# MLP of an encoder trunk in fp32: the up projection as seven block products on 256 tokens each, weight sums by accumulating DMAs, one block seeded in its PSUM bank

## The chip, the cores and the metric

One core of a Trainium2 chip. The time is that of one execution on the device in microseconds; lower is better. The kernel works in fp32: a product of fp32 numbers is made from three TensorE passes on rounded parts (fp32r): high x high, high x low, low x high.

## What is computed

Two layers of a bidirectional encoder, 512 tokens, width 1024, hidden width 4096. The part that the change concerns is the last line of a layer, with `hn` the normed input:

```python
hn = rms_norm(x, ln2[l])
x = x + jnp.square(jax.nn.relu(hn @ w_up[l])) @ w_down[l]
```

`hn @ w_up` is 512 x 1024 by 1024 x 4096, `@ w_down` 512 x 4096 by 4096 x 1024. Ahead of it in a layer stand the input projection, the three branches and the output projection `wo`; behind the last layer a final norm.

## The kernel before

**Splitting.** Weights come from DRAM in chunks of 128 x 1024 (512 KB). `wsplit` makes the two parts of a chunk: ScalarE casts it to `wh` (line 242), VectorE subtracts that from it into `wl` (line 243). There are three pairs of buffers `wh`/`wl` (`WB`). Activations are split in the same way by `split` (lines 307 and 308).

**MLP.** The hidden width is worked on in four quarters of 1024 (`qd`). A quarter has an up stage and a down stage.

- *Up*: for each of 8 tiles of 128 features, 8 k-tiles x 3 matmuls of 512 tokens (`proj`, lines 248 to 250), weights as the stationary operand, from tile `wr` (two buffers). ScalarE takes relu from PSUM (line 1319) and squares (line 1320).
- *Down*: the product is cut into 2 x 2 blocks (tokens, k, features) and made from seven block products instead of eight (a Strassen-Winograd scheme): `seven`, called with the numbers 1, 2, 6, 7, 5, 4, 3. Each has 4 k-tiles x 2 token tiles x 3 matmuls of 512 columns (lines 466 to 468). It needs sums of the activations' blocks, which `left_first`, `left_second` and `left_sums` make on VectorE during the up stage, and sums of weight blocks, made on VectorE: four in `early_sums` (lines 450 and 452), four in `seven` (lines 479 and 481). A quarter's weights lie in ten buffers of the pool `wq` (`uload`, line 228).
- The results of down are summed over quarters: 1 and 2 are read apart from banks "c" and "m", 1, 6, 5, 3 add up in "c", 7 and 4 in "a". `on` in `down` adds them to `acc` in SBUF (line 522), and in the last quarter to the residual `xr` (line 516), times r2 or -r2, the square of the norm's factor (relu and square let that factor be applied afterwards).

**Start of the MLP.** Transposes of the residual give the normed input by features (`norm_tok`, `turn`). The first three feature tiles begin on the first four k-tiles, so that the second half of the transposes comes among them.

**Order.** A scheduler places each instruction on its engine's queue by program order among what is ready, with `hp()` as a higher class; `tc.issue_after` fixes an order by hand. Engines run their queues in order. SP issues the loads of weights, POOL the DMAs of activations. Pools are opened and closed (`begin`, `end`) on the same memory: `wq` and `mlp` lie where `Y1` and `Y2` were, and `Y2` holds the operand of `wo`.

**Block products elsewhere.** The input projection uses `seven` too, with `uload` and `early_sums`.

Of the kernel before, what the change touches and what calls it, by code (L numbers as in the profile page):

```python
# [12 lines left out]
P = 128  # L13
S = 512
# [37 lines left out]
def _chunk_keys():  # L52

    res = []
    for l in range(DEPTH):
# [23 lines left out]
def trunk(tc, x0v, xT, xt, ws, fnb, bsb, snk, wst, rope, cmask, amask, ident, out):  # L79
# [4 lines left out]
    def pool(**kw):  # L84
# [18 lines left out]
             "h": 22}  # L103

    HOME = {t: p for p, ts in {"G": ("xs", "zt"), "Y1": ("yh",), "br": ("q", "a", "ao", "g", "ch"), "Y2": ("yi", "th", "mg"), "mlp": ("h",)}.items() for t in ts}
# [3 lines left out]
    WR, WB, NZ, NCT, NSM, NQ = 2, 3, 3, 4, 3, 10  # L109
# [110 lines left out]

    def uload(*key):

        raw = []
        for i in range(10):
            t = part["wq"].tile([P, CW], F32, tag="wq", bufs=NQ, name=nm("wq"))
            if i < 8:
                with hp():
                    d = nc.sync.dma_start(t, ws[CHUNK[key + (i // 2, i % 2)]])
                    if key == (0, "un", 0):
                        last_u[0] = d  # L230
            raw.append(t)
        return [raw[2 * q:2 * q + 2] for q in range(5)]
# [119 lines left out]
    def norm_tok(which, l, xr, keep, unit=1.0):  # L352
# [9 lines left out]
        def turn(fl, ts, banks="ssss"):  # L362
# [3 lines left out]
            for d in range(4 * fl, 4 * fl + 4):  # L366
                if n.xs[d] is None:
                    n.xs[d] = (T("x", "xh", F32R), T("x", "xl", F32R))
                    if keep:
                        n.xf[d] = Z() if d < 4 else T("l", "xf")  # L370
# [3 lines left out]
                src = pt[:, 0:w]  # L374
                parts = [x[:, c0:c0 + w] for x in n.xs[d]]
                if keep:
                    xf = n.xf[d][:, c0:c0 + w]
                    nc.scalar.activation(xf, src, AF.Copy, scale=ln_ap(which, l, d))
                    split(xf, *parts)
                else:  # L380
                    split(src, *parts, ln_ap(which, l, d))
# [23 lines left out]
    def left_first(new, u):  # L405

        p1 = new().rearrange("p (a b) -> p a b", a=2)
        split(u[:, 0:HT], p1[:, 0], p1[:, 1])
        sb_ = part["wq"].tile([P, 2, HT], F32, tag="sf", bufs=2, name=nm("sf"))
        i = nc.vector.tensor_tensor(sb_[:, 0], u[:, 0:HT], u[:, HT:], ALU.subtract)  # L410
        return {"i": i, 1: (p1[:, 0], p1[:, 1]), "u": u, "s": sb_}

    def left_second(new, h, v):
        V = nc.vector
        u, sb_ = h.pop("u"), h.pop("s")
# [1055 lines left out]
```

## Time and profile before

| | |
|---|---|
| median of 3 runs | 1628.48 us (1628.19 to 1629.73) |
| profiled execution | 1628.61 us, span 1626.8 us |
| granted TensorE clock | 0.997 |
| TensorE busy | 1606.8 us, 99% |
| VectorE busy | 1283.3 us, 79% |
| ScalarE busy | 993.3 us, 61% |
| POOL busy | 127.0 us, 8% |
| MLP of layer 0 | from 495.8 to 808.4 us of the span |
| MLP of layer 1 | from 1306.1 to 1618.6 us |

In the profile PE is TensorE's matmul, PEld its weight load, DVE is VectorE, ACT is ScalarE, SP and POOL issue DMAs. A matmul's duration (379 ns for 512 columns) holds the pipeline's depth; what it costs in a row is the distance from start to start. A row of operations gives line, engine, operation, output from inputs, count and the durations in ns (least, median, most, or the mean). In the table by stretch each engine has busy time and count of instructions; behind them stand the granted clock, the DMA engines' share and GB/s.

### The profile page before, as it was taken

The page shows a single profiled execution, that of the slowest core. Times are in us where ns is not written, and L with a number is a line of the kernel's source. Part 1 is how long each engine was busy: PE and PEld are TensorE (multiplying, and loading weights), DVE is VectorE, ACT ScalarE, POOL GpSimd, SP SyncE. Part 2 cuts the span into 40 slices and gives each one's busy share as a digit, 9 for nine tenths or more (in the row PEclk, how much of TensorE's full clock was granted, in tenths as well). Part 3 has the DMA queues.
Part 4 walks back from the last instruction along what each step waited for, and adds up shares of the span by engine and source line. Part 5 has one row for each costly group of instructions (what it writes and reads, how often), then busy time and mean ns, then how long its engine had stood idle before and what let it go on. Part 6 is the DMA issues. An engine that isn't in the chain of part 4 may idle for free.

```text
span 1626.8 us, 21854 instructions
## 1 busy us (share of the span) xinstructions
PE 1606.8 (99%) x8034; PEld 1413.0 (87%) x8034; DVE 1283.3 (79%) x1984; ACT 993.3 (61%) x1695; POOL 127.0 (8%) x185
## 2 busy tenths in 40 slices
PE   9999999999999999999999999999999999999998
PEld 8888888898888888888888888988888888888886
DVE  7996998685666768696989969977956677686967
ACT  7676678685245665545766667787852465545464
POOL 1021000001310000000010210000103000000000
PEclk9999999999999999999999999999999999999999
DMA  9342221222645323332423422212227453332321
GB/s 337 118 151 95 95 78 53 93 95 90 229 170 205 104 104 104 104 106 101 143 98 122 169 96 79 90 53 85 98 89 252 152 194 104 104 109 99 125 70 52
DMA packets 57115, 195.84 MB, mean 120 GB/s; under 512 B 7504, under 2 KB 7888, under 8 KB 57008
## 3 DMA queue, kind: packets, MB, share of 16 engines
q1 hardware_dynamic: 45216, 156.03, 27.7%
q0 software_dynamic: 11648, 38.15, 6.8%
q8 instruction: 63, 1.03, 0.3%
q14 instruction: 44, 0.36, 0.1%
q10 hardware_dynamic: 144, 0.26, 0.0%
HBM read 175.54 MB, written 18.87 MB: 120 GB/s over the span
## 4 chain that ended last, share of the span: by engine, by line
PE 74%; DVE 12%; issue 7%; ACT 5%; POOL 1%; DMA 1%; SPq 0%; POOLq 0%; DVEq 0%; ACTq 0%
PE up L249 7%; PE up L250 7%; PE up L248 7%; PE dA L466 3%; PE dA L468 3%; PE dA L467 3%; DVE ex L667 2%; DVE wl L243 2%; PE wo L300 2%; PE wo L299 2%; PE wo L301 2%; PE dC L466 2%; PE dC L467 2%; PE dC L468 2%; PE po L1109 2%
## 5 line engine op out<-in xcount | busy, mean ns | idle before, releaser
L242 ACT CAST wh<-wq 128x1024 fp32r<-128x1024 f32 x201 | 210.3, 1047 | 169.8 <-PE dA L467 43.0
L243 DVE TENSOR_TENSOR wl<-wq,wh 128x1024 fp32r<-128x1024 f32 x201 | 244.3, 1220 | 86.0 <-ACT wh L242 85.1
L243 DVE TENSOR_TENSOR wl<-wr,wh 128x1024 fp32r<-128x1024 f32 x166 | 203.3, 1225 | 127.8 <-ACT wh L242 122.4
L242 ACT CAST wh<-wr 128x1024 fp32r<-128x1024 f32 x166 | 173.4, 1045 | 208.5 <-PE up L249 57.8
L248 PE MATMUL up<-xh,wh 128*128 128x512 f32 x512 | 194.2, 379 | 0.0
L249 PE MATMUL up<-xl,wh 128*128 128x512 f32 x512 | 194.0, 379 | 0.0
L250 PE MATMUL up<-xh,wl 128*128 128x512 f32 x512 | 193.1, 379 | 0.0
L250 PEld LDWEIGHTS up<-xh,wl 128*128 128x128 f32 x512 | 96.8, 189 | 13.7
L248 PEld LDWEIGHTS up<-xh,wh 128*128 128x128 f32 x512 | 96.8, 189 | 13.7
L249 PEld LDWEIGHTS up<-xl,wh 128*128 128x128 f32 x512 | 96.8, 189 | 13.7
L466 PE MATMUL dA<-wh,sh 128*128 128x512 f32 x256 | 97.1, 379 | 0.0
L467 PE MATMUL dA<-wh,sh 128*128 128x512 f32 x256 | 97.0, 379 | 0.0
L468 PE MATMUL dA<-wl,sh 128*128 128x512 f32 x256 | 90.3, 379 | 0.0
L667 DVE TENSOR_TENSOR ex<-ex 128x512 f32<-128x512 f32 x112 | 79.2, 725 | 2.7 <-ACT key L647 2.7
L625 PE MATMUL at<-qt,kt 128*128 128x128 f32 x448 | 66.5, 281 | 3.9 <-DVE qt L640 2.0
L625 PEld LDWEIGHTS at<-qt,kt 128*128 128x128 f32 x448 | 60.7, 196 | 6.5 <-issue 3.1
L639 ACT ACTIVATE qt<-ex 128x512 f32<-128x512 f32 x56 | 37.5, 670 | 35.5 <-DVE ex L667 24.6
L307 ACT CAST sh<-sf 128x512 fp32r<-128x512 f32 x64 | 39.6, 619 | 24.8 <-DVE sf L430 17.7
L468 PEld LDWEIGHTS dA<-wl,sh 128*128 128x128 f32 x256 | 48.4, 189 | 6.8
L466 PEld LDWEIGHTS dA<-wh,sh 128*128 128x128 f32 x256 | 48.4, 189 | 6.8
L467 PEld LDWEIGHTS dA<-wh,sh 128*128 128x128 f32 x256 | 48.4, 189 | 6.8
L248 PE MATMUL gz<-xh,wh 128*128 128x512 f32 x128 | 49.3, 385 | 0.3 <-DVE gz L804 0.3
(417 smaller groups left out, 4297.9 us busy)
## 6 DMA issues: line engine op xcount, KB each, us to landing
wr<-in_ws_dram SPq DMA_DIRECT2D x166, 512.0 KB, 3.2
wq<-in_ws_dram SPq DMA_DIRECT2D x117, 512.0 KB, 4.3
thd<-zt POOLq DMA_DIRECT2D x32, 256.0 KB, 2.6
th<-thd POOLq DMA_DIRECT2D x32, 256.0 KB, 3.1
mgd<-mg POOLq DMA_DIRECT2D x16, 256.0 KB, 2.4
mB<-mgd POOLq DMA_DIRECT2D x16, 256.0 KB, 4.7
xt<-in_xt_dram SPq DMA_DIRECT2D x8, 256.0 KB, 7.5
xr<-in_xt_dram POOLq DMA_DIRECT2D x8, 256.0 KB, 4.9
```

The costliest lines, as they stand in the source:

```text
L242: cast_i[0] = nc.scalar.copy(hi, raw)
L243: nc.vector.tensor_tensor(lo, raw, hi.bitcast(F32), ALU.subtract)
L248: nc.tensor.matmul(o, whi, xh, start=first, stop=False)
L249: nc.tensor.matmul(o, whi, xl, start=False, stop=False)
L250: return nc.tensor.matmul(o, wlo, xh, start=False, stop=last)
L307: nc.scalar.copy(hi, src)
L466: nc.tensor.matmul(o, xh[:, t], h, start=start and k == 0, stop=False, skip_group_check=True)
L467: nc.tensor.matmul(o, xl[:, t], h, start=False, stop=False, skip_group_check=True)
L468: return nc.tensor.matmul(o, xh[:, t], l_, start=False, stop=k == 3, skip_group_check=True)
L625: nc.tensor.matmul(pt[:, c], kk(st), qq[:, c], start=True, stop=True)
L639: nc.scalar.activation(qt.rearrange(shp, b=nb, h=2), e_q, AF.Exp)
L667: nc.vector.tensor_tensor(o_ap, o_ap, ap_of(ex, i_, [[istep, 2]] + z), ALU.add)
```

## The change

- **Up** becomes block products too (`up` and `block_products` in place of the eight feature tiles; `seven` stays for the input projection). Blocks are 256 tokens x 512 k x 512 features. A product has 4 k-tiles x 4 feature tiles x 3 matmuls of 256 columns, the weights stationary. Its order is 7, 1, 2, 6, 5, 3, 4 (in a layer's first quarter 1, 7, 2, 6, 5, 3, 4). `w_up` is stored in chunks by blocks.
- **Activations.** The normed input gets its block sums in `put_x` and `sum_x`, once a layer. The up stage's `on` makes the four blocks of the hidden activations, and with product 4 the sums that down needs (`half`).
- **Weight sums**: a quarter's stage has a `Unit` with tiles b11, t3, b21, b22 (8 chunks; t3 has four buffers, the others two). t3 is loaded as b12 and has b22 added by a DMA on POOL's queue that accumulates in place; later steps add b11 to t3 (after 7), b12 to b11 and b21 to t3 (after 6). In up, except for the first quarter, the first two are accumulating DMAs; in down and in the first up stage b11 is added to t3 by VectorE and b12 to b11 by DMA. The third is VectorE's in all.
- **Seeded bank**: ScalarE copies product 1 from bank "c" to "m", and product 2 adds to it there.
- **Down**: its order is 1, 2, 7, 6, 5, 3, 4 (1, 2, 7, 6, 5, 4, 3 in the last quarter). `acc` goes: every quarter adds its products to `xr`.
- **Loads**: the next unit's chunks are loaded during this one, as buffers come free. Layer 1's first eight chunks are loaded behind the last down of layer 0 and their `early_sums` moves behind the end of the MLP.

```diff
-            res += [(l, "up", qd, f) for f in range(8)]
+            res += [(l, "up", qd, q, i) for q in range(4) for i in range(2)]
...
+        def add(self, what, q):
+            with hp():
+                for i in range(2):
+                    nc.gpsimd.dma_start(self.t[what][i], self.chunk(q, i), accum_op=ALU.add)
...
+    BANK = {1: "c", 2: "m", 7: "a", 6: "c", 5: "c", 3: "c", 4: "a"}
+    READ = {1: "P1", 2: "P12", 7: "P7", 6: "P16", 5: "P165", 3: "P1653", 4: "P74"}
+
+    def block_products(unit, order, product, on, nxt=None, by_dma=False, between=None, apart=False):
...
+        for n in order:
+            tag = BANK[n]
+            if n in (1, 7):
+                open_(tag)
+            raw = w[{1: "b11", 2: "b21", 7: "t3", 6: "t3", 5: "b11", 3: "b22", 4: "t3"}[n]]
+            pts, hl = banks[tag], []
+            tail = apart and n == order[-1]
+            for s_ in range(2):
+                with hp():
+                    hl.append(wsplit(raw[s_]))
+                if not tail:
+                    with tc.issue_after(turned.ins) if turned else contextlib.nullcontext():
+                        for p in range(2):
+                            mm = product(n, pts[p], p, (2 * s_, 2 * s_ + 1), hl[s_], n in (1, 7))
+                turned = between(mm) if between and n == order[0] and s_ == 0 else None
+            with hp():
+                if n == 7:
+                    if by_dma:
+                        unit.add("t3", 0)
+                    else:
+                        for i in range(2):
+                            V.tensor_tensor(w["t3"][i], w["t3"][i], w["b11"][i], ALU.add)
+                        unit.add("b11", 1)
+                elif n == 1 and by_dma:
+                    unit.add("b11", 1)
+                elif n == 6:
+                    for i in range(2):
+                        V.tensor_tensor(w["t3"][i], w["t3"][i], w["b21"][i], ALU.add)
+            if nxt:
+                for what in {order[2]: ("t3",), 6: ("b21",), 5: ("b11",), 3: ("b22",)}.get(n, ()):
+                    nxt.load(what)
...
+                    if n == 1:
+                        if p == 0:
+                            open_("m")
+                        nc.scalar.copy(banks["m"][p], pts[p])
+                    else:
+                        on(READ[n], p, pts[p])
...
+            r = r2 if sign > 0 else nr2
+            V.scalar_tensor_tensor(xr[t][fl], pt, r[:, t:t + 1], xr[t][fl], ALU.mult, ALU.add)
...
+    def up(qd, unit, nxt, xo, between):
...
+            for k in ks:
+                xh, xl = (ap_of(x, 0, [[1, P], [P, 2]]) for x in xo[k][n])
+                for j in range(2):
+                    c = (k % 2) * S + (2 * p + j) * P
+                    c = slice(c, c + P)
+                    o = by_two(pt[:, j * HT:(j + 1) * HT])
+                    nc.tensor.matmul(o, hl[0][:, c], xh, start=start and k + j == 0, stop=False, skip_group_check=True)
+                    nc.tensor.matmul(o, hl[0][:, c], xl, start=False, stop=False, skip_group_check=True)
+                    i = nc.tensor.matmul(o, hl[1][:, c], xh, start=False, stop=k == 3, skip_group_check=True)
...
+            elif which == "P74":
+                a21, a22, a11, a12 = (u[i, p] for i in (21, 22, 11, 12))
+                V.tensor_tensor(nat(a21), nat(a21), srt(pt), ALU.add)
+                A.activation(a21, a21, AF.Relu)
+                square(a21)
+                V.tensor_tensor(a22, a22, a21, ALU.subtract)
+                V.tensor_tensor(a21, a11, a21, ALU.subtract)
+                half(7, p, a21)
+                V.scalar_tensor_tensor(a11, a22, -1.0, a11, ALU.mult, ALU.subtract)
+                half(6, p, a11)
+                half(5, p, a22)
+                V.scalar_tensor_tensor(a12, a12, -1.0, a11, ALU.mult, ALU.subtract)
+                half(3, p, a12)
...
+        def sum_x():
+            V = nc.vector
+            for d in range(4):
+                u, v = xf[d], xf[d + 4]
+                a11, a21, a12, a22 = u[:, 0:HT], u[:, HT:], v[:, 0:HT], v[:, HT:]
+                sa = T("h", "sa")
+                V.tensor_tensor(sa[:, 0:HT], a22, a21, ALU.subtract)
+                V.scalar_tensor_tensor(sa[:, HT:], sa[:, 0:HT], -1.0, a11, ALU.mult, ALU.subtract)
+                a_ = T("x", "xh", F32R), T("x", "xl", F32R)
+                split(sa, *a_)
...
+                V.scalar_tensor_tensor(sd, a12, -1.0, sa[:, HT:], ALU.mult, ALU.subtract)
+                xo[d][3] = two(xb[d], 1)
+                split(sd, *xo[d][3])
```

More of the change, by code (lines that the diff above doesn't have):

```diff
@@ L447, in early_sums @@
     def early_sums(raw):
-        b11, b12, b22, b21, t1 = raw
+        b11, b12, b22, b21 = raw
+        t1 = [part["G"].tile([P, CW], F32, tag="t1", bufs=2, name=nm("t1")) for _ in range(2)]
+        raw.append(t1)
         for i in range(2):
@@ new lines, in down, with product @@
+    def down(qd, unit, nxt, hs, xr, r2, nr2, done, last):
+        V = nc.vector
+        def product(n, pt, p, ks, hl, start):
+            t = slice(p * P, (p + 1) * P)
+            for k in ks:
+                xh, xl = hs[k][n]
+                c = (k % 2) * S
+                o, h, l_ = by_two(pt), pairs(hl[0], c), pairs(hl[1], c)
+                nc.tensor.matmul(o, xh[:, t], h, start=start and k == 0, stop=False, skip_group_check=True)
+                nc.tensor.matmul(o, xl[:, t], h, start=False, stop=False, skip_group_check=True)
+                i = nc.tensor.matmul(o, xh[:, t], l_, start=False, stop=k == 3, skip_group_check=True)
+            return i
@@ L524, in down @@
-        if qd == 3:
-            for fl in range(2):
-                for t in range(4):
-                    V.scalar_tensor_tensor(xr[t][fl], acc[t][fl], r2[:, t:t + 1], xr[t][fl], ALU.mult, ALU.add)
-        seven(raw, hs, "d", on, apart=last and qd == 3)
+            r = r2 if sign > 0 else nr2
+            V.scalar_tensor_tensor(xr[t][fl], pt, r[:, t:t + 1], xr[t][fl], ALU.mult, ALU.add)
+            if qd == 3 and which in ("P12", "P165", "P74", "P1653"):
+                done(t, fl)
+        order = (1, 2, 7, 6, 5, 4, 3) if qd == 3 else (1, 2, 7, 6, 5, 3, 4)
@@ L1252, in trunk, with rest_of_norm @@
         begin("mlp")
+        unit = Unit(l, "up", 0)
+        for what in ("b11", "t3", "b21", "b22"):
+            unit.load(what)
+        def rest_of_norm(mm):
+            with hp():
+                with tc.issue_after(mm.ins):
+                    tp = n2.turn(1, range(4), "ssaa")
+                n2.end()
+                sum_x()
+            return tp
         last = l + 1 == DEPTH
         Z4("u")
-        n1 = norm_tok("ln1", l + 1, xr, True, 1.0 / math.sqrt(D) if last else 1.0)
-        acc = [[T("tv", "acc"), T("tv", "acc")] for _ in range(4)]
+        n1 = norm_tok("ln1", l + 1, xr, None, 1.0 / math.sqrt(D) if last else 1.0)
         fn_t, held = [], []
@@ L1332, in trunk @@
                         nc.sync.dma_start(fn_t[fl], bass.AP(tensor=fnb.tensor, offset=fnb.offset + fl * S, ap=[[0, P], [1, S]]))
-                else:
-                    nxt = uload(l + 1, "un", 0)
-            down(qd, raw, hs, acc, xr, r2, nr2, done, last)
+            down(qd, unit, nxt, hs, xr, r2, nr2, done, last)
+            unit = nxt
+        if not last:
+            nxt = uload(l + 1, "un", 0)
         if not last:
```

235 lines of the change are left out of this document (139 added, 96 removed).

## The prediction

> **What bounds the kernel now.** I read the page's first and fourth parts first, then a table of busy time by stretch of the MLP, then costs of single operations, then queues.
>
> ```profile
> span 1626.8 us, 21854 instructions
> PE 1606.8 (99%) x8034; PEld 1413.0 (87%) x8034; DVE 1283.3 (79%) x1984; ACT 993.3 (61%) x1695; POOL 127.0 (8%) x185
> PE 74%; DVE 12%; issue 7%; ACT 5%; POOL 1%; DMA 1%; SPq 0%; POOLq 0%; DVEq 0%; ACTq 0%
> ```
>
> TensorE is busy throughout and holds 74% of the chain that ends last; so matmul time taken away counts, if nothing else becomes late. Whether it does is a question to the stage that changes, the MLP. The table by stretch (length, then busy time and count of PE, PEld, DVE, ACT, POOL):
>
> ```profile
> 652.95:694.60 41.65, 41.65 (x194) 36.48 (x193) 26.53 (x40) 23.36 (x35) 0.00 (x0) 1.00 0.30 102
> 694.60:730.65 36.05, 36.05 (x169) 31.57 (x168) 33.37 (x41) 17.49 (x19) 0.00 (x0) 1.00 0.37 117
> 652.95:730.65 77.70, 77.70 (x362) 68.04 (x361) 59.90 (x81) 40.85 (x54) 0.00 (x0) 1.00 0.33 109
> 495.80:808.40 312.60, 312.60 (x1464) 273.86 (x1463) 242.81 (x333) 180.00 (x261) 4.36 (x7) 1.00 0.35 122
> 1306.10:1618.60 312.50, 312.50 (x1457) 273.66 (x1455) 239.93 (x318) 174.31 (x247) 1.73 (x2) 1.00 0.30 103
> ```
>
> The rows are an up stage, the down stage behind it, both (a quarter of a layer's MLP), and the MLP of each layer. A quarter's code has 192 + 168 = 360 matmuls of 512 columns; 77.70 / 360 = 0.216 us each, with no gap: the MLP runs at TensorE's pace. But VectorE (DVE) has 33.37 of 36.05 us in the down stage: 93%, the number to watch.
>
> **The change part by part.** *TensorE.* Up goes from 192 matmuls of 512 columns to 7 products x 4 k x 4 feature tiles x 3 = 336 of 256 columns, each with its own weight load. The nearest rows are two such matmuls of the attention scores between 512-column ones, and the weight loads beside them:
>
> ```profile
> 219.73 0.38 PE L248 MATMUL gz<-xh,wh 128*128 128x512 f32 x1
> 219.94 0.27 PE L1077 MATMUL sc<-k,q 128*128 128x256 f32 x1
> 220.05 0.28 PE L1077 MATMUL sc<-kl,q 128*128 128x256 f32 x1
> 220.16 0.38 PE L249 MATMUL gz<-xl,wh 128*128 128x512 f32 x1
> ```
>
> ```profile
> 219.73 0.19 PEld L1077 LDWEIGHTS sc<-k,q 128*128 128x128 f32 x1
> 219.95 0.19 PEld L1077 LDWEIGHTS sc<-kl,q 128*128 128x128 f32 x1
> 220.06 0.19 PEld L249 LDWEIGHTS gz<-xl,wh 128*128 128x128 f32 x1
> ```
>
> Start to start they take 0.11, and the loads keep that pace, running beside the matmul before. The run is short, so a longer one bounds it: 16 transposes of 128 columns with 16 loads.
>
> ```profile
> 498.39 1.91 PE L373 MATMUL xT<-id_t,xr 128*128 128x128 f32 x16
> ```
>
> Less a last one of 0.27, 1.64 / 15 = 0.109: a load is good for one every 0.109. I take 0.1095 (ends 0.109 and 0.112). Up: 336 x 0.1095 = 36.8 in place of 192 x 0.216 = 41.5. TensorE gains 4.7 a quarter, 37 in all; down keeps its 168 matmuls, 36.3.
>
> A rule that would speak against it stands in the Trainium skill, TensorE: Matmul & The Clock Gate, section The mechanism: weight loads overlap matmuls in flight only where the row groups differ; by it the 256-column matmul would cost load plus stream. The rows above contradict that (0.11 with a full load). The section LDWEIGHTS (loading the stationary operand) gives columns / 1.2, which is 107 ns, an estimate that agrees with 0.109.
>
> *VectorE and ScalarE.* Their costs:
>
> ```profile
> L242 ACT CAST wh<-wq 128x1024 fp32r<-128x1024 f32 x201 | 210.3, 1047 | 169.8 <-PE dA L467 43.0
> L243 DVE TENSOR_TENSOR wl<-wq,wh 128x1024 fp32r<-128x1024 f32 x201 | 244.3, 1220 | 86.0 <-ACT wh L242 85.1
> L1319 ACT ACTIVATE u<-up x64: 589/592/593, 508.8 to 1583.7; 128x512 f32<-128x512 f32 x64
> L1320 ACT ACTIVATE u<-u x64: 616/630/637, 509.5 to 1584.4; 128x512 f32<-128x512 f32 x64
> L307 ACT CAST sh<-sf x64: 607/618/627, 514.9 to 1589.0; 128x512 fp32r<-128x512 f32 x64
> L479 DVE TENSOR_TENSOR wq<-wq,wq x28: 1211/1220/1220, 39.3 to 1580.0; 128x1024 f32<-128x1024 f32 x28
> L516 DVE SCALAR_TENSOR_TENSOR xr<-dA,r,xr x16: 740/743/751, 778.6 to 1619.1; 128x512 f32<-128x512 f32 x16
> L430 DVE SCALAR_TENSOR_TENSOR sf<-sf,u x36: 418/420/426, 513.2 to 1586.5; 128x256 f32<-128x256 f32 x36
> L520 ACT ACTIVATE acc<-dA x12: 590/597/599, 544.1 to 1385.7; 128x512 f32<-128x512 f32 x12
> ```
>
> Independent VectorE operations start before the last is over:
>
> ```profile
> 698.85 1.22 DVE L243 TENSOR_TENSOR wl<-wq,wh 128x1024 fp32r<-128x1024 f32 x1
> 699.99 0.69 DVE L308 TENSOR_TENSOR sh<-u,sh 128x512 fp32r<-128x512 f32 x1
> 700.59 0.42 DVE L433 SCALAR_TENSOR_TENSOR sf<-u,sf 128x256 f32<-128x256 f32 x1
> 700.92 0.68 DVE L522 TENSOR_TENSOR acc<-acc,dA 128x512 f32<-128x512 f32 x1
> ```
>
> So one of 1024 elements occupies 1.14, of 512 0.60, of 256 0.33, and the update of xr about 0.66.
>
> VectorE's new up stage, its last product (4) left out: 14 weight splits instead of 8 (16.0), two sums of t3 and b21 (2.3), 8 operations of 512 for products 2, 5 and 3 (4.8): 23 us in TensorE's 36.8. Product 4 comes last and releases for each half nine operations of 512 (the sum with PSUM, a22, a21, a11, a12 and four splits): 18 x 0.60 = 10.8, which cannot begin before up's last matmuls end and so falls into the down stage. Down has 14 splits (16.0), four sums (4.6: the 7 and 6 steps keep VectorE) and 14 updates of xr (9.2): 29.8. Together 40.6 us in TensorE's 36.3. The stage idles VectorE for about 13 us and then overfills it by 4; the idle time cannot be used earlier, since three wh/wl buffers let splits run only one and a half products ahead.
>
> Where it waits: let T be up's last matmul. The splits for down's product 1 and half of product 2 are made or queued. The split of product 2's other half is cast when product 1's first half has freed a buffer, and TensorE needs it at T + 5.2 + 2.6 = T + 7.8. Product 4's operations are earlier in the program and have the same high priority, so they go first where both are ready. VectorE's queue: two splits (2.3), 18 operations (10.8), then this split (1.2), less about 1 done before T: T + 13.3. TensorE waits 5.5. ScalarE is not the cause: 14 casts (about 14), the two bank copies, and 7.5 of product 4 (relu, square and four casts, twice) in over 36 us.
>
> Two smaller waits. In down b11 gets its accumulating DMA after VectorE's sum has read it in step 7, and product 5's split waits for the landing. No accumulating DMA is in the trace; the nearest rows:
>
> ```profile
> wr<-in_ws_dram SPq DMA_DIRECT2D x166, 512.0 KB, 3.2
> xr<-in_xt_dram POOLq DMA_DIRECT2D x8, 256.0 KB, 4.9
> mC<-mcd POOLq DMA_DIRECT2D x8, 256.0 KB, 8.4
> ```
>
> Ends 3.2 and 8.4; I take 5, near the POOL queue's read from DRAM. From the sum to product 5 are some 10.4 us (products 7 and 6), less cast and split (2.3) and VectorE's lag: at 5 it costs 1.3 a quarter, at 3.2 nothing, at 8.4 about 4. In up, adds to t3 have products 1 and 2 (10 us) between them and their use; hidden up to about 8. The seeded bank's copy, 0.6 as L520's, has half a product of cover in both stages: 0 to 0.8, taken as 0.4 where it queues behind product 4's ScalarE work. A quarter: -4.7 + 5.5 + 1.3 + 0.4 = +2.5; eight of them +20.
>
> *Start of a layer's MLP.*
>
> ```profile
> SPq L228 <- PE wo L301: 2.4, 1, 2.4
> 495.99 3.40 SPq L228 DMA_DIRECT2D wq<-in_ws_dram x7
> DMA to landing us min/median/max: 3.1/7.0/9.3
> ```
>
> The wq pool's first load waits for the last wo matmul, T0. Before, that held up nothing, as up's weights are in wr. Now t3 lies there: load to T0 + 5, accumulating add (0.55 issue, 5) to T0 + 10.5, cast and split to T0 + 12.8. TensorE has product 1 and the transposes (5.3 + 1.8 = 7.1). Also sum_x and four splits go on VectorE ahead of product 7's split: 4 x (0.60 + 4 x 0.33 + 0.60), 10 us, from about T0 + 5.5, which is T0 + 16 and 1.2 for the split. The two overlap: 4 to 10, taken as 9; twice, +18.
>
> *The rest.* Layer 1's first eight loads and early_sums (4 x 1.14) move behind the last down: b12 and b22 wait for down's products 4 and 3, early_sums for the end of mlp's pool. They feed the second product, with bu's 96 matmuls (21 us) ahead of it; VectorE's queue there gets 4.6 longer: +2 (0 to 5). SP issues as many loads as before; a load waiting for its buffer holds those behind it, none needed within five us. POOL gets 10 adds a quarter (0.55 each, 5.5 of 80 us); an add waiting for its load holds up norm's power and xspill, neither needed soon. The removed updates of xr in the fourth quarter (8 x 0.66) fell under full TensorE: nothing.
>
> Sum against the profiled execution (1628.6, span 1626.8; the median 1628.48 is the same): 1628.6 + 20 + 18 + 2 = **1669 us**, slower.
>
> **The rivals.** *VectorE's burst is hidden (faster).* If at least nine of product 4's 18 operations stand behind the split of product 2's second half in the queue, the 5.5 goes; what is left is the sum, 40.6 less four updates that can run into the next up stage (2.6): 38.0, 1.7 over TensorE. A quarter then is -4.7 + 1.7 = -3.0; eight -24; the start with the t3 chain alone +11; 2: 1618. For it: these operations wait for ScalarE at first, and TensorE reached 93% VectorE without a gap before. Against: program order.
>
> *The accumulating DMAs are slow.* At 8.4 a quarter loses 2.7 more in down, and some in up: 8 x 3.3 = 26: 1695. For it: each reads the destination too and they queue in pairs on POOL. By the Trainium skill, DMA: Bandwidth & Descriptors, section Anatomy of one DMA, a fixed 2.0 us and 436 kB per us make 3.2 us for 512 KB, an estimate that is the wr row's; the section Rules for kernel authors says that an accumulate reads its destination first; no run yet shows its price.
>
> *The change does not speed TensorE up.* If sustained 256-column matmuls take 0.125 or more, up takes 42 us and the 4.7 is gone; with more time for VectorE in up, but the burst in down unchanged, 1669 + 37 = 1706. The skill's row-group rule leads this way; carried through (0.107 twice for each matmul) it would make 1669 + 8 x 35 = 1950, which the rows above leave no chance.
>
> **How the numbers follow.** Forecast 0.62 (its own range 1645 to 1695), hidden burst 0.22, slow DMAs 0.11, no gain on TensorE 0.05. The bounds of the terms taken all low reach 1640, so the range goes down to the second case: 1608 to 1702. No change and a small one cannot be told apart within about 0.2%. Of the second case 0.18 is faster by more than that, 0.03 within: faster 0.18, same 0.04, slower 0.78.
>
> **What would show it.** TensorE's up matmuls at 0.11 start to start; idle time on PE behind VectorE's weight split (wl) early in each down stage, some 5 us, none in the up stages after the first; VectorE over 95% busy in down, about two thirds in up; a gap of 4 to 10 us at the first product 7 of a layer; the accumulating DMAs' time to landing against 5. Wrong it would be if the splits go ahead of product 4's operations, or if the operations take less than these rows.

## The result, and the profile after

The changed kernel takes 1726.28 us (median; 1725.37 to 1728.42) beside 1628.62 for the kernel before, 1.060 times as long (95% interval 1.0582 to 1.0619): 98 us slower, where 40 were predicted. From the page of the changed kernel:

```profile
span 1725.2 us, 24564 instructions
PE 1619.4 (94%) x9186; PEld 1436.7 (83%) x9186; DVE 1351.8 (78%) x2012; ACT 1070.1 (62%) x1815; POOL 193.9 (11%) x261
PE 55%; DVE 24%; issue 9%; ACT 6%; DMA 5%; POOL 1%; SPq 0%; POOLq 0%; DVEq 0%; ACTq 0%
```

TensorE's share of the chain that ends last fell from 74% to 55%, VectorE's doubled, and DMAs, 1% before, have 5%. The table by stretch (length, busy time and count of PE, PEld, DVE, ACT, POOL, granted clock, DMA share, GB/s), for a later up stage, the down stage behind it, layer 0's first up stage, and the MLP of each layer:

```profile
598.60:636.20 37.60, 36.83 (x329) 36.56 (x328) 24.50 (x38) 27.72 (x41) 4.11 (x5) 1.00 0.74 190
636.20:683.70 47.50, 39.66 (x170) 32.15 (x168) 39.76 (x49) 22.33 (x29) 4.31 (x5) 0.96 0.54 135
499.30:549.50 50.20, 41.80 (x354) 41.30 (x353) 38.40 (x56) 36.98 (x60) 7.15 (x8) 0.90 0.83 232
499.30:856.96 357.66, 319.06 (x2047) 286.62 (x2046) 272.74 (x338) 215.85 (x315) 37.75 (x46) 0.95 0.64 166
1362.20:1717.25 355.05, 318.43 (x2033) 286.04 (x2031) 271.81 (x324) 209.74 (x299) 34.48 (x40) 0.95 0.59 150
```

The up stage does what was meant: 37.60 / 336 = 0.112 us a matmul. The down stage takes 47.50 in place of 36.05 for the same 168 matmuls, and VectorE is busy for 39.76 of it. The MLPs are 45.1 and 42.6 us longer than before; the remaining 11 lie ahead of the first (3.5) and between the two (7.5).

Inside the down stage, in four parts:

```profile
636.00:647.90 11.90, 11.90 (x58) 10.32 (x57) 11.87 (x18) 9.97 (x16) 0.86 (x1) 1.00 0.47 85
647.90:659.80 11.90, 8.50 (x35) 5.92 (x33) 11.90 (x16) 4.63 (x6) 1.73 (x2) 1.00 0.37 58
659.80:671.70 11.90, 7.77 (x27) 6.22 (x28) 7.41 (x8) 2.14 (x3) 0.00 (x0) 0.86 0.81 253
671.70:684.00 12.30, 11.95 (x57) 10.19 (x56) 9.09 (x10) 5.89 (x6) 1.73 (x2) 1.00 0.52 141
```

For 24 us VectorE has no gap, and in the second part TensorE stands because of it. In the third VectorE has gaps too (7.41), and the granted clock falls to 0.86: something else ends that wait. Rows picked from the timelines of the engines there (start, duration, engine; in brackets the idle time before and what ended it):

```profile
655.10 1.22 DVE L551 TENSOR_TENSOR t<-t,wr 128x1024 f32<-128x1024 f32 x1
656.99 0.86 POOL L261 DMA_DIRECT2D wr<-in_ws_dram  x1 [6.35 <-DVE sl L337]
662.81 1.04 ACT L271 CAST wh<-wr 128x1024 fp32r<-128x1024 f32 x1 [4.39 <-DMA wr<-in_ws_dram]
663.89 1.22 DVE L272 TENSOR_TENSOR wl<-wr,wh 128x1024 fp32r<-128x1024 f32 x1 [1.11 <-ACT wh L271]
665.03 1.40 DVE L592 SCALAR_TENSOR_TENSOR xr<-blkc,r,xr 128x512 f32<-128x512 f32 x2
665.92 0.59 PE L583 MATMUL blkc<-wh,sh 128*128 128x512 f32 x1 [3.37 <-DVE xr L592]
666.31 0.63 PE L584 MATMUL blkc<-wh,sl 128*128 128x512 f32 x1
```

Read from the top: VectorE's second sum of t3 and b11, late behind product 4's work; b12's accumulating DMA, which may overwrite b11 only after it; its landing 5.8 us after the issue; the cast; the split, for which VectorE's queue waits 1.11; behind the split the updates of xr that read bank "c", which product 5's matmul needs. After 3.37 us of standing TensorE's matmuls are 0.43 apart for nine matmuls instead of 0.216: from 665.92 on, nine take 3.7 us instead of 1.9.

### The profile page after: what moved, and what is told of

Read it like the earlier page. It is cut to its first block, busy times and chain, and to the rows that moved or that the text cites. A ratio compares the mean times of both kernels' runs of the same rounds, so it can differ in the third digit from the quotient of the medians.

```text
span 1725.2 us, 24564 instructions
## 1 busy us (share of the span) xinstructions
PE 1619.4 (94%) x9186; PEld 1436.7 (83%) x9186; DVE 1351.8 (78%) x2012; ACT 1070.1 (62%) x1815; POOL 193.9 (11%) x261
## 4 chain that ended last, share of the span: by engine, by line
PE 55%; DVE 24%; issue 9%; ACT 6%; DMA 5%; POOL 1%; SPq 0%; POOLq 0%; DVEq 0%; ACTq 0%
DVE wl L272 7%; DMA wr<-in_ws_dram 3%; PE blkc L613 3%; PE blkc L612 3%; PE blkc L611 3%; DVE sl L337 2%; PE blkc L583 2%; ACT wh L271 2%; PE blkc L584 2%; PE blkc L585 2%; DVE ex L814 2%; PE at L772 2%; PE wo L328 2%; PE wo L329 2%; PE wo L330 2%
## 5 line engine op out<-in xcount | busy, mean ns | idle before, releaser
L271 ACT CAST wh<-t 128x1024 fp32r<-128x1024 f32 x146 | 152.7, 1046 | 106.0 <-PE blkc L584 60.4
L272 DVE TENSOR_TENSOR wl<-t,wh 128x1024 fp32r<-128x1024 f32 x146 | 178.1, 1221 | 46.9 <-ACT wh L271 46.7
L272 DVE TENSOR_TENSOR wl<-b,wh 128x1024 fp32r<-128x1024 f32 x103 | 125.6, 1222 | 46.8 <-ACT wh L271 46.0
L271 ACT CAST wh<-b 128x1024 fp32r<-128x1024 f32 x103 | 107.7, 1045 | 84.3 <-PE blkc L584 41.8
L583 PE MATMUL blkc<-wh,sh 128*128 128x512 f32 x256 | 107.5, 420 | 31.8 <-DVE xr L592 23.4
L585 PE MATMUL blkc<-wl,sh 128*128 128x512 f32 x256 | 103.1, 420 | 13.6 <-DVE wl L272 13.6
L584 PE MATMUL blkc<-wh,sl 128*128 128x512 f32 x256 | 104.8, 409 | 0.0
L337 DVE TENSOR_TENSOR sl<-u,sh 128x512 fp32r<-128x512 f32 x112 | 75.5, 685 | 12.4 <-ACT sh L336 12.4
L585 PEld LDWEIGHTS blkc<-wl,sh 128*128 128x128 f32 x256 | 53.5, 209 | 27.8 <-DVE wl L272 19.1
L611 PE MATMUL blkc<-xh,wh 128*128 128x256 f32 x256 | 70.1, 275 | 0.0
L612 PE MATMUL blkc<-xl,wh 128*128 128x256 f32 x256 | 70.1, 275 | 0.0
L786 ACT ACTIVATE qt<-ex 128x512 f32<-128x512 f32 x56 | 37.6, 672 | 34.9 <-DVE ex L814 24.9
```

The source lines that it names most:

```text
L271: cast_i[0] = nc.scalar.copy(hi, raw)
L272: nc.vector.tensor_tensor(lo, raw, hi.bitcast(F32), ALU.subtract)
L337: return nc.vector.tensor_tensor(lo, src, hi.bitcast(F32), ALU.subtract)
L583: nc.tensor.matmul(o, xh[:, t], h, start=start and k == 0, stop=False, skip_group_check=True)
L584: nc.tensor.matmul(o, xl[:, t], h, start=False, stop=False, skip_group_check=True)
L585: i = nc.tensor.matmul(o, xh[:, t], l_, start=False, stop=k == 3, skip_group_check=True)
```

## The experiments

One run each, unless an interval is given. Stage lengths go from a stage's first matmul to the next stage's. "Down" is the mean of the six down stages that do not end a layer (47.9 us in the changed kernel), "first up" the first up stage of each layer (50.2 and 50.5).

### What holds the down stage

**Without b12's accumulating DMA.**

```diff
-                        unit.add("b11", 1)
+                        pass
```

> Leaves out the accumulating DMAs that turn b11 into b11 + b12 (block product 5's weight) in the down stages and in the first up stage of a layer; product 5 there multiplies by b11 alone. Theory A (a down stage lasts 47.5 us instead of 36.3 because VectorE's burst of product 4's work delays the weight sum, the accumulating DMA is issued behind that sum, and TensorE waits 3.4 us for its landing and then runs some nine matmuls at half clock): the 3.4 us and about 1 of the clock go, a down stage takes 43 to 44 us, eight of them give 28 to 36 us, total 1690 to 1698 us. Rival V (VectorE's backlog alone sets the stage, the DMA's wait only covers it): the wait turns into waits for VectorE's splits, a down stage stays at 46.5 or more, total 1718 or more.

1707.99 us, down 45.1: between the two. The stage as above, in this run:

```profile
633.50:678.17 44.67, 37.99 (x171) 31.05 (x169) 39.73 (x49) 22.37 (x29) 2.59 (x3) 1.00 0.44 120
660.01 1.23 DVE L557 TENSOR_TENSOR t<-t,b 128x1024 f32<-128x1024 f32 x1
661.14 1.41 DVE L592 SCALAR_TENSOR_TENSOR xr<-blkc,r,xr 128x512 f32<-128x512 f32 x2
662.04 0.45 PE L583 MATMUL blkc<-wh,sh 128*128 128x512 f32 x1 [2.17 <-DVE xr L592]
```

The same gap is still 2.17 us, now ended by VectorE's own queue, and the clock stays at 1.00. So here the DMA costs 1.2 us of gap and 1.8 of clock on top of a backlog of VectorE that is there without it. In the other stages half clock does not go away altogether: the granted clock of the six down stages is 0.93, 0.96, 0.96, 0.93, 0.93 and 0.93 in the changed kernel, and 0.96, 1.00, 0.96, 0.96, 0.96 and 1.00 in this run.

**A shorter burst.**

```diff
-                half(5, p, a22)
-                V.scalar_tensor_tensor(a12, a12, -1.0, a11, ALU.mult, ALU.subtract)
-                half(3, p, a12)
+                for k in (2 * p, 2 * p + 1):
+                    hs[k][5] = hs[k][3] = hs[k][6]
```

> Leaves out the last three VectorE operations (and two ScalarE casts) of product 4's chain in each half of an up stage: a12's sum and the splits for block products 5 and 3, which use product 6's tiles instead. That is 3.6 us less of VectorE at the head of each down stage. Theory A: everything behind the burst, the sum and the accumulating DMA with it, comes 3.6 us earlier: a down stage takes 44 us, total about 1698 (1694 to 1704). Rival D (the DMA alone sets the wait, from a point that the burst does not move): a down stage stays at 47, total 1720 or more. Rival V (VectorE's own total bounds the stage): also 3.6 less a stage, about 1698, so this run tells D from the other two, and the run without b11's DMAs tells A from V.

1696.42 us, down 44.2: 3.6 us less of VectorE shorten the stage by 3.6, and the DMA's gap stays (4.1 us in front of product 5). This rules out D; the two runs together say that the burst carries the DMA with it.

**Product 4 ahead of product 3 in up.**

```diff
-            block_products(unit, (7, 1, 2, 6, 5, 3, 4), product, on, nxt, by_dma=True)
+            block_products(unit, (7, 1, 2, 6, 5, 4, 3), product, on, nxt, by_dma=True)
```

with a12's sum and split behind product 3, and the same swap in the first up stage.

> Same computation as the changed kernel; in the up stages block product 4 runs ahead of product 3, so that product 4's burst (some 11 us of VectorE) starts one product, 5.4 us, earlier and lies under product 3; product 3's own chain, with a12's sum and split, comes last. Theory A: 5.4 of the burst's 11 us leave the down stage, the sum and the accumulating DMA come that much earlier: a down stage takes 42 to 44 us, total 1686 to 1700. Rival H (down's second product needs product 3's half, now the last to be split, behind the burst): a wait of 2 to 5 us moves there, a down stage takes 45 to 47 us, total 1706 to 1722.

1691.13 us, down 44.7: A's total, though the stage lies 0.7 above A's range and just below H's. Waits of 2.6 us in all did move towards the head of the stage, three gaps of which the longest is 1.63, but in front of product 7, not of the second product as H has it; they are smaller than the gain.

**The accumulation priced.**

```diff
-                    nc.gpsimd.dma_start(self.t[what][i], self.chunk(q, i), accum_op=ALU.add)
+                    nc.gpsimd.dma_start(self.t[what][i], self.chunk(q, i))
```

> The changed kernel with each accumulating DMA turned into a plain copy of the same chunk to the same tile from the same queue at the same time, so that the weights' sums that they form are left out: prices the accumulation itself. If the accumulation is what makes these DMAs take 7.5 to 7.8 us where SyncE's plain loads of the same 512 KB take 3.5 to 4.4: they land in 4 to 5 us, the wait in front of product 5 falls below what VectorE's backlog leaves (2.2 us, no half clock), as in the run without these DMAs, total about 1708. If it is POOL's queue: they stay at 7 us or more, and the total at 1722 or more.

1710.92 us, down 45.1, like the run without b12's DMA, though half clock did not go (granted clock 0.93 in the stage shown for the other runs). Rows of the page's DMA part (count, size, median us from issue to landing), first of the changed kernel with the plain load of SP, then of this run:

```profile
wr<-in_ws_dram SPq DMA_DIRECT2D x134, 512.0 KB, 3.5
t<-in_ws_dram POOLq DMA_DIRECT2D x44, 512.0 KB, 7.8
wr<-in_ws_dram POOLq DMA_DIRECT2D x32, 512.0 KB, 7.5
```

```profile
t<-in_ws_dram POOLq DMA_DIRECT2D x44, 512.0 KB, 4.8
wr<-in_ws_dram POOLq DMA_DIRECT2D x32, 512.0 KB, 3.8
```

From the same queue, to the same tiles, the accumulation itself costs 3.0 to 3.7 us in these medians; POOL's queue costs little. But the medians mix stages. b12's adds alone, in the down stage shown above and in the up stage behind it, and then the plain copies in the same two stages of this run:

```profile
wr<-in_ws_dram POOLq DMA_DIRECT2D x2, 512.0 KB, 5.6
wr<-in_ws_dram POOLq DMA_DIRECT2D x2, 512.0 KB, 11.7
```

```profile
wr<-in_ws_dram POOLq DMA_DIRECT2D x2, 512.0 KB, 3.7
wr<-in_ws_dram POOLq DMA_DIRECT2D x2, 512.0 KB, 5.0
```

Where TensorE waits for it, in down, the accumulation adds 1.9 us. The 11.7 us in up cost nothing: that stage stays at 37.6 us. The Trainium skill, DMA: Bandwidth & Descriptors, section Rules for kernel authors, says that an accumulate reads its destination and writes it later; it has no price, and these rows give one.

**Down in up's manner**, on top of product 4 first.

```diff
-        order = (1, 2, 7, 6, 5, 4, 3) if qd == 3 else (1, 2, 7, 6, 5, 3, 4)
-        block_products(unit, order, product, on, nxt, apart=last and qd == 3)
+        order = (7, 1, 2, 6, 5, 4, 3)
+        block_products(unit, order, product, on, nxt, by_dma=True, apart=last and qd == 3)
```

> Same computation; the kernel with product 4 ahead of product 3 in the up stages, and with the down stages in the up stages' manner as well: order 7, 1, 2, 6, 5, 4, 3, b11 added to t3 and b12 to b11 by accumulating DMAs issued right behind the casts of products 7 and 1, so that VectorE's two sums a stage (1.22 us each) go and no accumulating DMA is queued behind VectorE. Theory B (down stages lose time to VectorE's total, 38.7 to 39.8 us of work against 36.3 of matmuls, and to the landing behind it): VectorE has about 36.3 us left, the gap of 2.95 us in front of product 5's weight and its half clock go, a down stage takes 38 to 41 us instead of 45; total 1691 less 8 times 4 to 7, 1635 to 1659 us. Rival P (product 7's operand, the first that product 4's chain gives, is late, and the two more accumulating DMAs on POOL's queue are late as well): a down stage stays at 43 or more, total 1675 or more.

1658.05 us, down 39.2: 5.6 us less a stage.

```profile
628.46:667.41 38.95, 37.50 (x169) 31.40 (x170) 34.47 (x42) 21.34 (x28) 5.21 (x6) 1.00 0.71 177
```

TensorE is busy for 37.50 of 38.95 and VectorE has room. The two accumulating DMAs no longer wait for a sum on VectorE. Of the 11.8 us that a down stage was above the old 36.05, 8.7 are gone. This run takes VectorE's sums and the DMA's late issue away at once, so it does not divide the 5.6 us between them; what holds the last 3 us was not tried, apart from the next run.

**The last sum of down by DMA too.**

```diff
+                elif n == 6 and order[-1] == 4:
+                    unit.add("t3", 3)
```

> Same computation; the same as the run before with the last sum of the down stages (t3 + b21, for product 4) by accumulating DMA too, in three quarters of four, with product 3 ahead of product 4 there so that the DMA has two products' time: 2.44 us of VectorE less a stage, two DMAs of 7.8 us more. Theory B: VectorE falls to some 34 us, below the 36.3 us of matmuls; a down stage is 1 to 2.4 us shorter than in the run before, total lower by 6 to 14 us. Rival Q (POOL's queue or the traffic now sets it): the DMA is late for product 4, a down stage is as long or longer, total the same or up to 20 us higher.

1657.35 us, down 39.0. VectorE fell to 33.0 us as expected, but the gain of 6 to 14 us did not come: after the run before, VectorE's total was no longer the limit.

### What holds the first up stage

In the changed kernel, the waits of 505 to 520 us (engine and line, what they waited for, us, times, longest), and what follows:

```profile
PE blka L611 <- ACT wh L271: 8.4, 1, 8.4
ACT wh L271 <- DMA t<-in_ws_dram: 2.8, 1, 2.8
```

```profile
507.00:515.00 8.00, 0.06 (x1) 0.06 (x1) 7.61 (x19) 5.67 (x11) 0.87 (x1) 0.63 1.04 295
515.00:519.00 4.00, 3.96 (x17) 3.67 (x18) 2.61 (x3) 1.31 (x2) 0.86 (x1) 0.50 0.66 202
```

While TensorE stands, VectorE is busy with the norm's sums and splits (7.61 of 8.00) and the DMA engines are full (1.04); then TensorE works at half clock. Both explanations fit.

**Without t3's add there.**

```diff
-            if what == "t3":
+            if what == "t3" and self.key[1:] != ("up", 0):
                 self.add("t3", 2)
```

> Leaves out the accumulating DMAs that form t3 = b21 + b22 in the first up stage of a layer (t3 there is the one chunk that the plain load brings). In that stage TensorE stands 8.4 us in front of product 7 and then runs at a granted clock of 0.50 for some 4 us; the stage takes 50.2 us instead of 37.6. Theory T (the chain load, accumulate, cast sets the 8.4 us): the first up stage falls to 41 or 42 us, total about 1708 (1704 to 1712). Rival X, the one the prediction named beside it (sum_x's VectorE work of the norm holds the split of t3 until nearly the same time): at most 2 us a layer, total 1722 or more.

(t3 is b12 + b22; the text names it wrongly.) 1724.17 us, first up 47.8 and 48.9, X's number. The 8.4 us in front of product 7 do go, but waits of 2.7 and 1.6 for the norm's splits take their place.

**Product 2 second, the norm's sums at ordinary priority**, on top of down in up's manner.

```diff
-            block_products(unit, (1, 7, 2, 6, 5, 4, 3), product, on, nxt, between=between)
+            block_products(unit, (1, 2, 7, 6, 5, 4, 3), product, on, nxt, between=between)
```

with `sum_x()` taken out of `hp()`.

> Same computation; the kernel with down in up's manner (order 7, 1, 2, 6, 5, 4, 3), and in the first up stage of a layer product 2 second and product 7 third, with the norm's sums for products 5, 6 and 3 at ordinary priority instead of ahead of the weights' splits. Theory X (in that stage sum_x's VectorE work holds the split of t3, and a standstill over 3 us costs half clock besides): the 8.4 us wait shrinks to 3 or less and the half clock with it, the stage falls from 50 to 41 to 44 us, total 12 to 18 us below the same kernel without it. Rival Y (the norm's second half, which product 2 needs, or the sums themselves come too late for the third or fourth product): the wait only moves, the stage stays over 47, total within 6 us.

1657.98 us, first up 49.1 and 53.5: Y. The waits stand in front of products 2, 7 and 5 now.

**t3 summed by VectorE, and the norm's sums by GpSimd.** The first of these two has product 2 second as well, the loads of t3 replaced by `nc.vector.tensor_tensor(t3, b21, b22, ALU.add)`; the second moves the three sums of `sum_x` to `nc.gpsimd`. Unlike what the two texts say ("Same computation"), both leave b12 out of t3.

> Same computation; the kernel with all weight sums of the down stages by accumulating DMA, and in the first up stage of a layer: order 1, 2, 7, 6, 5, 4, 3, t3 = b21 + b22 by VectorE (two sums of 1.22 us from tiles that are loaded anyway) in place of two plain loads and two accumulating DMAs of t3, and the norm's sums at ordinary priority. Theory X' (that stage is held by both: the chain of t3's loads and accumulating DMAs, and VectorE's 39.7 us of work in a stage of 37.6 us of matmuls): t3 is there when product 2 ends, the 2.86 us gap in front of product 5 shrinks too since the sums behind product 7 start some 4 us earlier; the stage takes 41 to 44 us instead of 50.5, total 1657 less 13 to 19: 1638 to 1644 us. Rival V (VectorE alone: 2.44 us more on it): the stage stays at 47 or more, total 1650 or more.

> Same computation; the run before with the norm's twelve 256-column sums on GpSimd instead of VectorE (some 5.1 us off VectorE, one split in two). Rival V: another 3 to 5 us off the stage, total 6 to 10 us below the run before. Theory X' with the chain gone: VectorE no longer bounds at 42 us, at most 2 us a layer; GpSimd's sums, taken as half of its 1.72 us for 512 columns, end some 11 us after the norm's factors, before product 6 needs them, total 0 to 4 us below. If GpSimd is slower than that, product 6 waits and the total rises.

1648.26 us, first up 47.3 and 49.1; and 1659.23, first up 53.5 and 53.2. In the first the stage is as long as V says, though the total is below V's. The second lost 11 us: GpSimd's sums of 256 columns took 0.98 to 1.32 us in the mean where 0.86 was assumed, and products 2, 7 and 6 waited.

**t3 summed in turn, and the same without the norm's sums.**

```diff
+                    if n == 7 and unit.key[1:] == ("up", 0):
+                        V.tensor_tensor(raw[s_], raw[s_], w["b22"][s_], ALU.add)
                     hl.append(wsplit(raw[s_]))
```

> Same computation; all weight sums of the down stages by accumulating DMA, and in a layer's first up stage: order 1, 2, 7, 6, 5, 4, 3, t3 loaded plainly as b12 and b22 added to it by VectorE just ahead of product 7's split, the norm's sums at ordinary priority. (The two runs before summed b21 and b22 there instead, so they left b12 out of t3; the sizes and the number of the operations were the same but for the two plain loads.) In those runs TensorE stood 2.3 us in front of product 2, whose split stood behind the two sums of t3, and ran at a granted clock of 0.69 after it. With the sums in turn that goes: the stage 43 to 46 us instead of 47.3 and 49.1, total 1640 to 1646 us. If VectorE, busy without a gap for 24 us there, sets the stage whatever the order: the same 1647 to 1650. Either way some 1% slower than the kernel before the change, which has the first up stage in 38 us.

> The run beside it with the norm's sums for products 5, 6 and 3 left out (these products take the tiles of products 2 and 7): 9.5 us less of VectorE and 5.8 us less of ScalarE in a layer's first up stage, nothing else changed. If VectorE's work bounds that stage: its gaps go, the stage takes 39 to 41 us, total 6 to 12 us below the run beside it. If the chain of loads and accumulating DMAs bounds it: within 3 us of it.

1651.93 us (ratio 1.0146 to the kernel before, 1.0129 to 1.0162), first up 49.2 and 50.3; without the norm's sums 1653.07, first up 51.8 and 49.8. So VectorE's work alone does not set the stage either: with 7.1 us less of it (34.42 us busy in layer 0's stage instead of 41.56; the 9.5 counted overlapping operations in full), a wait behind b12's DMA and half clock fill the time. (The 38 us given for the kernel before end at its first down matmul; its last up matmuls run on to 539.4, 43.6 us after the start.) The waits of the run without the sums at 505 to 530 us, and the stretch after them; the copy that product 5 waits for (L648) stands on ScalarE's queue behind the cast that waits for the DMA:

```profile
ACT wh L271 <- DMA wr<-in_ws_dram: 4.6, 2, 3.5
PE blkc L615 <- ACT u L648: 4.3, 1, 4.3
```

```profile
529.70:533.70 4.00, 4.00 (x20) 4.00 (x20) 1.60 (x2) 1.04 (x2) 0.00 (x0) 0.50 0.51 153
```

**Both taken away**: without the norm's sums, and without b12's DMA in the first up stage.

> The kernel without the norm's sums (products 5, 6 and 3 take the tiles of products 2 and 7), and in the first up stage b12's accumulating DMA to b11 left out too. Theory X' (two limits of nearly the same size, each of which hides the other: VectorE's work, and b12's DMA behind the next stage's two t3 adds): with both gone the 4.3 and 3.1 us in front of product 5 go and the half clock behind them; the stage takes 41 to 44 us instead of 51.8 and 49.8, total 1653 less 12 to 20: 1633 to 1641. If a third limit stands behind them (the norm's casts, the plain loads): 46 or more, total 1645 or more.

1638.69 us, first up 43.4 and 44.9.

```profile
497.85:541.26 43.41, 40.57 (x353) 39.60 (x351) 34.16 (x42) 33.90 (x54) 6.26 (x7) 1.00 0.78 235
```

The gaps in front of product 5 are gone, and the stage is about as long as in the kernel before (43.6). That is X': two limits of nearly the same size, and taking one away shows the other. The fourth combination, with the norm's sums but without b12's DMA, was run only on the changed kernel, where t3's chain is a limit too: leaving the DMA out there left the first up stages at 50.2 and 51.2.

**The next stage's t3 later.**

```diff
-                for what in {order[2]: ("t3",), 6: ("b21",), 5: ("b11",), 3: ("b22",)}.get(n, ()):
+                for what in {order[2] if by_dma else 0: ("t3",), 6: ("b21",) if by_dma else ("t3", "b21"), 5: ("b11",), 3: ("b22",)}.get(n, ()):
```

> The kernel without the norm's sums, b12's accumulating DMA kept, but the next stage's t3 (plain load and accumulating DMA) issued behind product 6 instead of product 7, so that b12's adds are no longer queued behind two others. Queue theory: b12's adds land in 7 to 8 us instead of 9 or more, the gap in front of product 5 falls to 1 to 2 us with no half clock, the stage 43 to 47 us, total 1638 to 1647. If the DMA's own length sets the wait whatever the queue holds: within 3 us of 1653.

> Same computation; the version with t3's sum in turn, with the next stage's t3 issued behind product 6 in a layer's first up stage. Theory X': b12's DMA is out of the way but VectorE's work still bounds, so the gaps of 1.5 us in front of product 5 shrink a little: the stage 46 to 49 us instead of 49.2 and 50.3, total 1643 to 1651. If the next down stage then waits for its t3, which is its first product: the gain is lost there, 1650 to 1656.

1652.74 and 1653.15 us (ratio 1.0132 to 1.0166). These tell nothing of the queue: the scheduler issued the loads and adds in the order they had before, so the runs repeat those they were set beside (1653.07 and 1651.93) to within 1.2 us. They show how far one stage scatters, though: without the norm's sums the first up stages are 48.3 and 51.7 here, 51.8 and 49.8 there, with gaps in front of product 5 of 3.5 and 6.3 here, 4.3 and 3.1 there. A difference of 3 us in one stage of one run says nothing. The next pair orders the adds with `tc.issue_after` on b12's last add.

> The kernel without the norm's sums, with the next stage's two t3 adds ordered behind b12's two adds on GpSimd's queue in a layer's first up stage (so far they were issued 3.7 us ahead of them). Queue theory: b12's adds land 3 to 4 us earlier, the gap of 4.3 and 3.1 us in front of product 5 falls to 1 or less, no half clock follows it; the stage 43 to 46 us instead of 51.8 and 49.8, total 1636 to 1644, as with b12's adds left out (1638.7). If b12's DMAs need their 8 to 9 us whatever is queued ahead: within 3 us of 1653.

> Same computation; the version with t3's sum in turn (1652 us), with the same order of the adds. VectorE's work with the norm's sums is still there, 24 us without a gap, so its second sum of t3 and b11, on which b12's second add waits, still comes at 521 us, 4 us later than without the norm's sums: the gain is smaller, the stage 46 to 49 us, total 1644 to 1652.

1652.21 us, first up 48.7 and 50.5; and 1653.23 (ratio 1.0131 to 1.0165), first up 49.5 and 51.8, above the stage and the total that were expected. The adds of the run without the norm's sums:

```profile
514.64 0.94 POOL L264 DMA_DIRECT2D wr<-in_ws_dram  x1 [13.76 <-DVE t L558]
518.20 0.86 POOL L264 DMA_DIRECT2D wr<-in_ws_dram  x1 [2.62 <-ACT sh L341]
518.80 2.02 POOL L264 DMA_DIRECT2D t<-in_ws_dram  x2
```

b12's adds now go first, and the cast that waits for the second still starts at 525.65, 7.4 us after its issue; with the old order it started 9.2 us after. The gaps are 3.9 and 3.8 us, where they were 4.3 and 3.1. The queue theory falls, and its rival stands: the issue behind a sum of VectorE and the 7.4 us to landing together are longer than products 7 and 6.

No version of these beat the kernel before. The best that computes everything, the one with t3 summed in turn, has MLPs of

```profile
498.62:819.44 320.82, 307.66 (x2051) 281.12 (x2050) 258.04 (x327) 216.98 (x319) 47.77 (x57) 0.99 0.81 205
1321.01:1641.35 320.34, 305.78 (x2033) 280.37 (x2031) 256.40 (x313) 209.38 (x300) 44.77 (x52) 0.99 0.76 186
```

beside 312.60 and 312.50: TensorE is busy 5 to 7 us less than before, and some 13 to 14.5 us of gaps have come in, about half of them in the first up stage.

## Why the prediction was wrong

The direction held, and so did the outline: TensorE gains in up, VectorE overflows in down, the stage waits. The step that failed is the burst's wait in the down stage. It was put in front of product 2, at 5.5 us; it is 8.6 us and lies in front of products 7, 6 and 5. And the half clock that follows idle time of TensorE was no term of the sum at all.

- **TensorE in up** ("36.8 in place of 41.5"): 37.6. The pace is 0.112, the upper end given, so the gain is 4.1 a quarter (41.65 less 37.60), not 4.7.
- **The burst** ("TensorE waits 5.5"): this is the step that failed most. VectorE's total was right (40.6 predicted, 39.76 busy). The order in its queue was not. Three rows of the stage:

```profile
640.28 1.22 DVE L272 TENSOR_TENSOR wl<-b,wh 128x1024 fp32r<-128x1024 f32 x1
652.90 0.48 PE L584 MATMUL blka<-wh,sl 128*128 128x512 f32 x1 [1.31 <-DVE sl L337]
656.23 0.69 DVE L337 TENSOR_TENSOR sl<-u,sh 128x512 fp32r<-128x512 f32 x1
```

  The first is the split of product 2's second half. The prediction had it behind all 18 operations of product 4, at T + 13.3; it comes 4.2 us after up's last matmul (636.1), with four of the 18 ahead of it. The last of the other fourteen is the third row. That is what the prediction itself named as a sign of being wrong. So product 2 does not wait (no gap reaches 0.7 us before 650 us), and the backlog comes out later, at products 7, 6 and 5: 8.6 us a stage, the run without b12's DMA (44.67) less 36.05. There it costs more than an overflow of 4 to 5 us, because a product also waits for the updates of xr that empty the bank it adds to, and these stand in VectorE's one queue behind sums and splits (the row at 662.04). That these two ways of waiting make the difference is read from the rows, not tested by itself.
- **b11's DMA** ("5, near the POOL queue's read from DRAM", 1.3 a quarter): 2.8 a stage (47.50 less 44.67). The landing was not the error: b12's adds landed after 5.4 to 6.2 us in the medians of the eight down stages, close to the 5, counted from the start of the issue. The gap that the DMA adds, 1.2 us (3.37 less 2.17), is close to the 1.3 too. What was left out is the half clock behind the longer gap.
- **Half clock** is the term that was missing. Nine matmuls at 0.43 in the down stage shown are 1.8 us, more than half of what the DMA costs there. In the first up stage TensorE works at half clock from 514.94 to 519.3, which costs about 2.2.
- **The seeded bank** (0.4 a quarter): product 2's first weight load waits 0.2 us for the copy and its matmuls do not.
- **Start of a layer's MLP** ("4 to 10, taken as 9"): the wait is 8.4, near the 9, and the half clock behind it makes the stage 50.2 and 50.5 where the terms gave 47.6 (36.8 + 1.8 of transposes + 9). That t3's chain and sum_x overlap was right; in the versions with product 2 second a third party showed, b12's DMA.
- **The rest** (2): 11. Part of it is not run-to-run scatter: in 18 runs with the same order of matmuls up to there, layer 0's MLP starts at 497.0 to 500.9, always later than the 495.8 before. Which of the moved weight sums costs it was not tried.

By these rows a quarter costs -4.1 + 8.6 + 2.8 = +7.3, not +2.5. Eight of them make 58; the first up stages are 12.6 and 12.9 above the 37.6 of the others, less 1.8 each for the transposes that were there before, 22; with 11 outside the MLPs 91 of the 98. The other 7 lie in single stages, 2.7 of them in layer 0's last down stage (50.2). Of the 58 us between the forecast and the result, the burst's wait is the largest part, 25 (eight times 8.6 less 5.5).

The hidden burst (1618) is refuted, though its condition came true: more than nine of product 4's operations did stand behind the split of product 2's second half, and the 5.5 in front of that product went. The stage still did not fall to VectorE's total less four updates, 38.0; without b12's DMA it takes 44.67. Two rivals come nearer to the measured time than the forecast, and both by luck. The one of slow DMAs (1695) had 8.4 us to landing in down, where 5.6 were measured. The one in which TensorE gains nothing (1706) is refuted by 0.112; so is the row-group rule weighed there, now for 336 matmuls in a row.

## What to carry to other kernels

Before a term is sized, follow what stands behind a late instruction in the same in-order queue: here an accumulating DMA queued behind a VectorE sum held up VectorE's next split, the updates behind it and, through the bank, TensorE. Count TensorE's idle time, not only its longest gap: in the changed kernel about 2 us of it within one step of 3.41 us, in one gap or in several, brought half clock for the next 3.41 us, which costs up to 1.7 us more. When taking away one limit moves nothing, take away two together before the theory is given up: the first up stage fell by 5 to 8 us only then. And a median over all stages can mislead: the accumulating DMA's 7.5 us was 5.6 where it was waited for.

## What the runs showed of the hardware

The clock after idle time: at half clock matmuls of 512 columns came 0.43 us apart instead of 0.216, and matmuls of 256 columns 0.21 instead of 0.11. In all 19 traces the half clock comes in stretches of 3.41 us, or two or three times that (a stretch in which the kernel ends is cut short), and within a trace they start whole multiples of 3.41 us apart. Some steps of this grid as a table by stretch, first in the changed kernel, then in the run without b12's DMA:

```profile
570.54:573.95 3.41, 1.40 (x5) 0.95 (x6) 3.41 (x5) 1.60 (x2) 0.87 (x1) 1.00 0.56 79
573.95:577.36 3.41, 3.28 (x8) 2.02 (x7) 1.95 (x2) 0.87 (x1) 0.00 (x0) 0.50 1.00 294
662.70:666.11 3.41, 0.19 (x1) 0.22 (x2) 2.30 (x4) 1.99 (x2) 0.00 (x0) 1.00 0.86 304
666.11:669.52 3.41, 3.41 (x9) 2.66 (x9) 1.46 (x2) 0.00 (x0) 0.00 (x0) 0.50 0.89 275
669.52:672.93 3.41, 3.41 (x17) 2.98 (x17) 1.05 (x2) 1.13 (x2) 0.00 (x0) 1.00 0.24 96
```

```profile
656.70:660.12 3.42, 2.00 (x8) 1.43 (x8) 3.42 (x4) 0.42 (x1) 0.00 (x0) 1.00 0.43 165
660.12:663.53 3.41, 1.49 (x7) 1.36 (x8) 3.41 (x4) 0.62 (x1) 0.00 (x0) 1.00 0.90 265
663.53:666.95 3.42, 3.42 (x18) 2.99 (x17) 0.91 (x2) 0.96 (x1) 0.00 (x0) 1.00 0.88 337
```

In the first row TensorE is busy for 1.40 us of 3.41, and no gap is longer than 1.30; the next step has half clock. In the third row the gap of 3.37 us leaves 0.19; the next step has half clock, the one after it is full again. In the other run the gap of 2.17 us, with one of 1.90 before it, leaves 2.00 and 1.49 us of busy time in the two steps that they fall into, and the clock stays. So the length of a gap does not decide, but the idle time that falls into one step: another gap of 2.17 us in that same run (in front of 1430.87) is followed by half clock. In the changed kernel, from 100 us on, every step at full clock with up to 1.47 us of busy time was followed by half clock and none with 1.60 or more. Over all 19 traces the border is less sharp: between 1.45 and 1.74 us both happened.

The Trainium skill, TensorE: Matmul & The Clock Gate, section What's actually happening, has half clock after an idle window of about 3.4 us that runs freely, without regard to the kernel. The trace agrees with the half, with the length and with the free running. The window need not be idle throughout: 1.40 us of work in it did not keep the clock up here.

An accumulating DMA of 512 KB from GpSimd's queue took 5.6 us to land in the down stage shown and 11.7 in the up stage behind it, a plain one from the same queue 3.7 and 5.0. What makes it slower in up was not tried.
